# Two weight sums a stage later, a copy behind the norm, and a second buffer for the second sums

## The chip, the cores and the metric

The kernel runs on one core of a Trainium2 chip. The core has a matrix engine (TensorE, PE in the profile; its weight loads are the row PEld), a vector engine (VectorE, DVE), a scalar engine (ScalarE, ACT), a general engine (GpSimd, POOL) and DMA queues, which here are mostly filled by SyncE (SP). The metric is the time of one execution on the device in microseconds.

## What is computed

One layer of a hybrid backbone for 1024 latent tokens of width 1024, with 256 context tokens in front. Cut to what matters here:

```python
y_m = mlstm_merge(hm, om, mlstm_norm[l])                        # mLSTM heads, 512 columns
y_a = window_attention(q, k, v, k_ctx, v_ctx, attn_sink[l])     # 8 query heads, 512 columns
x = x + g_a * (concatenate([y_m, y_a]) @ w_out[l])              # the projection
h = modulate(rmsnorm(x, norm_ffn[l]), sh_f, sc_f)               # the norm
a, val = split(h @ w_up[l], 2)                                  # up projection, 2 x 2816 columns
x = x + g_f * ((gelu(dwconv(a)) * val) @ w_down[l])             # down projection
out = rmsnorm(x, final_norm)
```

## The kernel before, in words

Large matmuls are done in float32 by splitting each operand into a high part (a rounded copy, `fp32r`) and a low part (the difference), and adding three products. A split is therefore two steps: a copy, mostly on ScalarE, and a subtraction on VectorE (line 1193, the helper `sub`).

**Order.** From the attention on, the order of the work on TensorE, VectorE, ScalarE and GpSimd is that in which the program writes it (`manual_schedule`); each engine goes through its own list in order and waits where an input or a buffer is not ready. Lists of small steps, `more[t, i]`, are hung into the attention at stage t, place i, and run by `fill`.

**The attention** goes over 32 pairs (8 blocks of 128 tokens, 2 key heads, 2 pairs of query heads each), one pair per stage t, as a pipeline: at stage t, pair t has its scores made, pair t - 1 is normalised on GpSimd (`nrm`, line 1142), pair t - 2 is transposed on TensorE (`tr`, line 1154), copied (`hi`, line 1161), its low part made (`lo`, line 1167, tile `pl`) and multiplied with the values (`pv`, line 1177, tile `u`), and pair t - 3 finishes its products and is put together into `yT` (`y1`, lines 1182 and 1183; `y2`, lines 1188 and 1189). `u` has one buffer, so the next pair's `pv` waits for `y2`. Stages n = 32 and n + 1 only empty the pipeline. Beside it run the projection's products of the mLSTM half (`Wout`; its `add` is line 1092). At stage n, place 3, ahead of the pair's `pv`, VectorE makes three sums (lines 1252 and 1193) over the four quarters of block 0's up weights, which a DMA has put into `ym`; they go into `yS`, a part of the tile `yT`.

**The projection** of the attention half then goes over the tiles `order = [4, 1, 5, 2, 6, 3, 7]`; tile 0 was done in the attention. For each tile: 24 matmuls in two halves (`wout_n`, lines 307 to 309), an add to x (line 1383), the squares (`sq`, line 1393) and root (line 1398) on ScalarE, a reciprocal (line 1402) and the norm (`norm_b`, lines 1404, 1405 and 1407), transposes (`trans`, line 1419) and a move out of PSUM with scale and shift (`evac`, lines 1430 and 1432). The inputs `yT` of the tiles are split by `ysplit_h` and `ysplit_l`; the parts of the first three tiles have buffers of their own (`yh`, `yl`, three each), those of the others lie in free places of `hB`, the big pair of tiles for the up projection's token side.

**The up projection** multiplies 2 x 2 halves of tokens and of channels by seven products instead of eight, on sums and differences of the halves. The token sums of tile b and its partner b - 4 are `sum1` to `sum4`, split into the blocks T1 to T4 of `hB` (`split_t1` to `split_t4`, line 1443 for the copy); the plain blocks are B11, B21 and B22. `sum2` writes a tile `tb` of its own, which has one buffer and is read by `split_t2` and `sum4`. For tiles 6 and 7 (`late` and `last` in the code, with their partners 2 and 3), these steps stand after the loop, among the splits of block 0's weight sums (`wsplit_h`, line 1587). Behind them come five products of block 0, in this order: pf, pc (T1), pb (T2), pe (T3), pd (T4), and then block 1's.

Of the kernel before, what the change touches and what calls it, by code (L numbers as in the profile page):

```python
# [9 lines left out]
F32 = mybir.dt.float32  # L10
F32R = mybir.dt.float32r
# [7 lines left out]
P = 128  # L19
# [59 lines left out]
def build(tc, I, out, dbg=None):  # L79
    nc = tc.nc  # L80
    dbg = dbg or {}
    V, S, G, T = nc.vector, nc.scalar, nc.gpsimd, nc.tensor
# [41 lines left out]
    ym = rp.tile([P, NL, 512], F32, name="ym")  # L124
# [5 lines left out]
    hl = [hl_(0)]  # L130
# [13 lines left out]
    def load_split(src, w, rawf=None, split=True, alloc=True, now=range(2)):  # L144
        room = lambda: [st.tile([P, KT, XW], F32R, name=n, tag=n)[:].rearrange("p a b -> p (a b)")[:, :KT * w]
                        .rearrange("p (k f) -> p k f", k=KT) for n in ("wh", "wl")]
        hi, lo = room() if alloc else (None, None)
        raws = {}

        def load(q):  # L150
            raws[q] = rawf() if rawf else sr.tile([P, 4, XW], F32, name="wr", tag="wr")
            nc.sync.dma_start(raws[q][:, :, :w], src[:, 4 * q:4 * q + 4, :])

        def cut(q):
            ks, raw = slice(4 * q, 4 * q + 4), raws[q]
            S.copy(hi[:, ks, :w], raw[:, :, :w])
            V.tensor_tensor(out=lo[:, ks, :w], in0=raw[:, :, :w], in1=hi[:, ks, :w].bitcast(F32), op=ALU.subtract)

        if split:
            for q in range(2):  # L160
                load(q)
                cut(q)
            return hi, lo
        for q in now:
            load(q)

        def rest(qs=range(2)):
            nonlocal hi, lo
            if hi is None:
                hi, lo = room()  # L170
            for q in qs:
                cut(q)
            return hi, lo
        rest.load = load
        return rest
# [296 lines left out]
    order = (list(range(NCH)), [1, 0] + list(range(NCH - 1, NC - 1, -1)))  # L472
# [486 lines left out]
    n = 0  # L959
# [12 lines left out]
    for h in range(H):  # L972
# [3 lines left out]
        else:  # L976
            wq = [wkq]
            late = lambda: wq.append(load_split(I["w_q"][1], 256, lambda: pq.tile([P, 4, 256], F32, name="wr", tag="rga")))
# [66 lines left out]
    yslice = lambda b: next(v[:, t.index(b)] for t, v in yTa.items() if b in t)  # L1045
# [3 lines left out]
    t4 = pb_.enter_context(tc.tile_pool(name="t4", bufs=2, reuse_waits="tile"))  # L1049
# [7 lines left out]
    class Wout:  # L1057
# [32 lines left out]
        def add(self, n):  # L1090
            ns = slice(512 * n, 512 * n + 512)
            V.tensor_tensor(out=self.xb[:, ns], in0=self.po[:], in1=self.xb[:, ns], op=ALU.add)
            if n == 1:
                nc.sync.dma_start(x2_d[self.b][:], self.xb[:])
# [96 lines left out]
    order = [4, 1, 5, 2, 6, 3, 7]  # L1191
    ys = {}
    sub = lambda e, o, x, y: e.tensor_tensor(out=o, in0=x, in1=y, op=ALU.subtract)  # L1193

    def ysplit_h(b, eng=G, room=None):
        ys[b] = room or [t4.tile([P, 4, P], F32R, name=f"y{n}", tag=f"y{n}", bufs=3)[:] for n in "hl"]
        eng.copy(ys[b][0], yslice(b)) if eng is S else eng.tensor_copy(ys[b][0], yslice(b))

    def ysplit_l(b):
        sub(V, ys[b][1], yslice(b), ys[b][0].bitcast(F32))  # L1200
# [13 lines left out]
    more = collections.defaultdict(list)  # L1214
# [28 lines left out]
    n = len(pairs)  # L1243
# [4 lines left out]
    more[n - 5, 2] += [lambda: ysplit_l(order[0])]  # L1248
    more[n - 4, 0] += [lambda: ysplit_h(order[1], S)]
    more[n - 3, 0] += [lambda: ysplit_l(order[1])]  # L1250
    more[n - 2, 0] += [lambda: ysplit_h(order[2], S)]
    add = lambda e, o, x, y: e.tensor_tensor(out=o, in0=x, in1=y, op=ALU.add)
    yS = yTa[2, 0, 4, 1, 5][:].rearrange("p w k t -> p w (k t)")

    def load_0(to, h):
        nc.sync.dma_start(to, I["w_up"][0, :, 2 * h:2 * h + 2].rearrange("p q k f -> p q (k f)"))

    more[n - 11, 0] += [lambda: load_0(ym[:, 2:4], 0), lambda: load_0(ym[:, 4:6], 1)]
    more[n, 3] += [lambda: add(V, yS[:, 2], ym[:, 5], ym[:, 4]), lambda: sub(V, yS[:, 3], yS[:, 2], ym[:, 2]),
                   lambda: sub(V, yS[:, 1], ym[:, 3], yS[:, 3])]  # L1260

    attn = tc.manual_schedule(engines={mybir.EngineType.PE, mybir.EngineType.DVE, mybir.EngineType.Activation,
                                       mybir.EngineType.Pool})
# [4 lines left out]
    for t in range(n + 2):  # L1268
# [3 lines left out]
        if t in WOT:  # L1272
            k = 4 + WOT.index(t)
            room = [wop.tile([P, D], F32R, name=f"wo{n}{k}")[:] for n in "hl"]
# [70 lines left out]
    hB = [hbp.tile([P, 7, 4, 512], F32R, name=f"hB{i}") for i in range(2)]  # L1345
    tbk = ExitStack()
    tbp = tbk.enter_context(tc.tile_pool(name="tbp", bufs=1, side="right", reuse_waits="tile"))
    B11, B21, B22, T1, T2, T3, T4 = range(7)
# [19 lines left out]
    hns, rs, pts, raws, tbs = ({} for _ in range(5))  # L1368
    last = order[-1]
# [15 lines left out]
    def mean0(b):  # L1385
        V.tensor_scalar(out=rs[b][:, 2:3], in0=rs[b][:, 0:1], scalar1=1.0 / D, scalar2=EPS, op0=ALU.mult, op1=ALU.add)

    def sq(b, n, mean=True):
        if n == 0:
            hns[b] = t5.tile([P, D], F32, name="hn", tag="hn")  # L1390
            rs[b] = t5.tile([P, 3], F32, name="r2", tag="r2")
        ns = slice(512 * n, 512 * n + 512)
        S.activation(hns[b][:, ns], xs[b][:, ns], AF.Square, accum_out=rs[b][:, n:n + 1])
        if n == 1:
            if mean:
                run(1)
                mean0(b)
            S.activation(rs[b][:, 0:1], rs[b][:, 1:2], AF.Sqrt, bias=rs[b][:, 2:3], scale=1.0 / D)

    def norm_b(b, halves=False):  # L1400
        run(1)
        V.reciprocal(rs[b][:, 0:1], rs[b][:, 0:1])
        if halves:
            S.activation(hns[b][:, 0:512], xs[b][:, 0:512], AF.Copy, scale=rs[b][:, 0:1])
            V.tensor_scalar(out=hns[b][:, 512:D], in0=xs[b][:, 512:D], scalar1=rs[b][:, 0:1], scalar2=None, op0=ALU.mult)
        else:
            S.activation(hns[b][:], xs[b], AF.Copy, scale=rs[b][:, 0:1])
# [28 lines left out]
    def run(n=99):  # L1436
        for _ in range(min(n, len(held))):
            held.pop(0)()

    def split(b, blk, w, src, hi_eng=S):  # L1440
        ts = slice(b % 4 * P, b % 4 * P + P)
        hi, lo = (hB[i][:, blk:blk + w, :, ts] for i in range(2))
        (S.copy if hi_eng is S else hi_eng.tensor_copy)(hi, src)  # L1443
        return lambda: sub(V, lo, src, hi.bitcast(F32))


    def sum1(b):
        sub(V, raws[b - 4][:, 0], raws[b][:, 0], raws[b - 4][:, 0])

    def sum2(b):  # L1450
        tbs[b] = tbp.tile([P, 1, 4, P], F32, name="tb", tag="tb", bufs=1)
        sub(V, tbs[b][:, 0], raws[b][:, 1], raws[b - 4][:, 0])

    def sum3(b, e=V):
        sub(e, raws[b][:, 0], raws[b][:, 1], raws[b][:, 0])

    def sum4(b, e=V):
        sub(e, raws[b - 4][:, 1], raws[b - 4][:, 1], tbs[b][:, 0])

    split_b = lambda b: split(b, B22, 1, raws[b][:, 1:2])  # L1460
    split_t1 = lambda b: split(b, T1, 1, raws[b - 4][:, 0:1])
    split_t2 = lambda b: split(b, T2, 1, tbs[b][:])
    split_t3 = lambda b: split(b, T3, 1, raws[b][:, 0:1])
    split_t4 = lambda b: split(b, T4, 1, raws[b - 4][:, 1:2])
# [10 lines left out]
    add = lambda e, o, x, y: e.tensor_tensor(out=o, in0=x, in1=y, op=ALU.add)  # L1475
# [3 lines left out]
    fence.__enter__()  # L1479
    sq(0, 0)  # L1480
    sq(0, 1)
    for j in range(3, 7):
        ysplit_h(order[j], G, [hB[n][:, B22 + j - 3, :, 3 * P:4 * P] for n in range(2)])
    for j in range(2, 5):
# [3 lines left out]
    late = None  # L1488
    for i, b in enumerate(order):
# [20 lines left out]
        if pp is not None and pp < 4:  # L1510
# [4 lines left out]
            late = None  # L1515
            run(1)
        if pp is not None and pp >= 4:
# [6 lines left out]
            late = pp  # L1524
# [11 lines left out]
    evac(prev)  # L1536
    add1()
    late = pp
    lo_b = split_b(late)
    mean0(last)  # L1540
    lo3 = split(prev, B11, 2, raws[prev][:], V)
    sq(last, 1, False)
    sum1(late)
    norm_b(last, True)
    lo3()
    prod(ps_a, e0, 0, B11, True, True, None, c3)
    prod(ps_a2, e0, 1, B21, True, False, None, c3, range(2))
# [14 lines left out]
    f = ExitStack()  # L1562
# [20 lines left out]
    def wsplit_h(R, n):  # L1583
        src = (R[0] and R[0][:], R[1][:, 2:4], R[1][:, 0:2] if R[0] else r1[:], R[1][:, 4:5] if R[0] else yS[:, 1:2])[n]
        w = src.shape[1]
        wt = [fw.tile([P, w, 512], F32R, name=f"w{n}{w}", tag=f"w{n}{w}", bufs=5 if w == 2 else 2) for n in "hl"]
        S.copy(wt[0][:], src)  # L1587

        def lo():
            sub(V, wt[1][:], src, wt[0][:].bitcast(F32))  # L1590
            return wt
        return lo
# [5 lines left out]
    lo_b = split_b(last)  # L1598
# [9 lines left out]
    lo_2 = split_t2(late)  # L1608
    wS = wS()
    S.copy(ar0[:], ps_a[:])  # L1610
    lo_1()
    lo_2()
    sum3(late)
    sum4(late)
    sum2(last)
    lo_3, lo_4 = split_t3(late), split_t4(late)
    lo_2 = split_t2(last)
    wA = wsplit_h(R, 2)
    lo_2()
    sum3(last)  # L1620
    lo_5 = split_t3(last)
    lo_3()
# [8 lines left out]
                                                                    tag={"a": "a", "f": "b", "b": "b"}.get(n, "c"))  # L1631
# [118 lines left out]
    for i in range(1, NF):  # L1750
        last = i == NF - 1
# [175 lines left out]
    more = {}  # L1927
# [87 lines left out]
    for t, (p, ps, fresh) in enumerate(products):  # L2015
        for j in range(NP):
            n = NP * t + j
# [34 lines left out]
            if NP + 3 <= n < NP + 3 + NL:  # L2052
                b = n - NP - 3
# [17 lines left out]
    n = len(steps) - 3  # L2071
# [100 lines left out]
```

## Time and profile before

| | us |
|---|---|
| median of three runs | 1273.13 (1272.91 to 1273.3) |
| the profiled execution | 1274.79 |
| its span, first to last instruction | 1273.0 |
| TensorE busy | 1238.7 (97%) |
| VectorE busy | 974.5 (77%) |
| ScalarE busy | 638.0 (50%) |
| GpSimd busy | 188.0 (15%) |
| mean granted clock of TensorE | 0.997 |

Times in the profile count from the span's first instruction. A line of a timeline has the start, the duration, the engine, the line of the program, the operation, its output and inputs, shapes, and in brackets the engine's idle time before it with what ended that. The attention ends near 585 us, the projection near 630 us, and the up projection's own loop begins near 652 us. The projection's products before 585 us at lines 307 to 309 belong to the mLSTM half.

### The profile page before, as it was taken

The page shows a single profiled execution, that of the slowest core. Times are in us where ns is not written, and L with a number is a line of the kernel's source. Part 1 is how long each engine was busy: PE and PEld are TensorE (multiplying, and loading weights), DVE is VectorE, ACT ScalarE, POOL GpSimd, SP SyncE. Part 2 cuts the span into 40 slices and gives each one's busy share as a digit, 9 for nine tenths or more (in the row PEclk, how much of TensorE's full clock was granted, in tenths as well). Part 3 has the DMA queues.
Part 4 walks back from the last instruction along what each step waited for, and adds up shares of the span by engine and source line. Part 5 has one row for each costly group of instructions (what it writes and reads, how often), then busy time and mean ns, then how long its engine had stood idle before and what let it go on. Part 6 is the DMA issues. An engine that isn't in the chain of part 4 may idle for free.

```text
span 1273.0 us, 19254 instructions
## 1 busy us (share of the span) xinstructions
PE 1238.7 (97%) x7047; PEld 1062.6 (83%) x7047; DVE 974.5 (77%) x1691; ACT 638.0 (50%) x1309; POOL 188.0 (15%) x162
## 2 busy tenths in 40 slices
PE   6999999999999999999999999999999999999997
PEld 4799998989898888887877888888888888788886
DVE  4873687868787888788987877777777776867887
ACT  6732556464765877775844333333333333434435
POOL 1200000000000443221002331232231232001000
PEclk9999999999999999999999999999999999999999
DMA  9541544453255333104413322333322337975553
GB/s 356 186 125 35 142 129 145 117 170 92 79 166 171 133 117 117 51 33 136 146 50 116 115 100 92 108 108 108 108 99 91 108 119 268 342 255 179 196 194 135
DMA packets 90560, 176.17 MB, mean 138 GB/s; under 512 B 12954, under 2 KB 29538, under 8 KB 90466
## 3 DMA queue, kind: packets, MB, share of 16 engines
q1 hardware_dynamic: 90178, 174.15, 40.6%
q8 instruction: 56, 0.92, 0.3%
q10 hardware_dynamic: 288, 0.79, 0.2%
q14 instruction: 38, 0.31, 0.1%
HBM read 136.58 MB, written 38.33 MB: 137 GB/s over the span
## 4 chain that ended last, share of the span: by engine, by line
PE 76%; DVE 9%; ACT 6%; DMA 5%; issue 2%; POOL 1%; SPq 0%; ACTq 0%; DVEq 0%; POOLq 0%
PE pd L2009 14%; PE pa L1471 8%; PE pc L1471 8%; PE pp L588 7%; PE pe L1471 4%; PE pd L1471 4%; PE pb L1471 4%; PE u L1177 3%; PE pt L1154 2%; PE pv L307 2%; PE pv L309 2%; PE pv L308 2%; PE po L307 1%; PE po L309 1%; PE po L308 1%
## 5 line engine op out<-in xcount | busy, mean ns | idle before, releaser
L1587 ACT CAST wh<-Rb 128x1024 fp32r<-128x1024 f32 (+1 forms) x63 | 56.8, 904 | 144.4 <-PE pd L1471 77.3
L2009 PE MATMUL pd<-dh,al 128*128 128x512 f32 x296 | 115.4, 390 | 0.9 <-DVE al L1352 0.9
L2009 PE MATMUL pd<-dl,ah 128*128 128x512 f32 x296 | 115.3, 389 | 0.0
L2009 PE MATMUL pd<-dh,ah 128*128 128x512 f32 x296 | 115.1, 389 | 0.0
L1471 PE MATMUL pc<-hB,wh 128*128 128x512 f32 x344 | 105.6, 389 | 0.0
L1471 PE MATMUL pa<-hB,wh 128*128 128x512 f32 x336 | 103.7, 390 | 0.3 <-ACT sn L1668 0.2
L1193 DVE TENSOR_TENSOR wl<-Rb,wh 128x1024 fp32r<-128x1024 f32 (+1 forms) x63 | 65.8, 1046 | 39.2 <-ACT wh L1587 38.7
L1704 POOL TENSOR_TENSOR tt<-vt,tt 128x512 f32<-128x512 f32 x22 | 29.6, 1343 | 368.5 <-ACT tt L1698 368.5
L588 PE MATMUL pp<-hl,wh 128*128 128x512 f32 x256 | 79.3, 405 | 0.0
L307 PE MATMUL pv<-wh,hl 128*128 128x256 f32 x256 | 76.1, 297 | 0.8 <-ACT ym L601 0.8
L1471 PEld LDWEIGHTS pc<-hB,wh 128*128 128x128 f32 x344 | 64.6, 188 | 13.4
L1471 PEld LDWEIGHTS pa<-hB,wh 128*128 128x128 f32 x336 | 62.9, 188 | 14.1 <-ACT sn L1668 1.1
L309 PE MATMUL pv<-wh,hl 128*128 128x256 f32 x256 | 72.3, 283 | 0.0
L308 PE MATMUL pv<-wl,hl 128*128 128x256 f32 x256 | 72.3, 282 | 0.0
L2009 PEld LDWEIGHTS pd<-dh,al 128*128 128x128 f32 x296 | 55.6, 188 | 13.2 <-DVE al L1352 1.6
L1471 PE MATMUL pc<-hB,wl 128*128 128x512 f32 x172 | 66.4, 389 | 0.0
L1471 PE MATMUL pa<-hB,wl 128*128 128x512 f32 x168 | 65.4, 389 | 0.0
L2009 PEld LDWEIGHTS pd<-dl,ah 128*128 128x128 f32 x296 | 55.6, 188 | 11.7 <-DVE dl L1352 0.3
L2009 PEld LDWEIGHTS pd<-dh,ah 128*128 128x128 f32 x296 | 55.6, 188 | 11.6
L1161 ACT CAST ph<-pt 128x512 fp32r<-128x512 f32 (+1 forms) x88 | 46.2, 525 | 28.2 <-PE pt L1154 28.0
L1471 PE MATMUL pb<-hB,wh 128*128 128x512 f32 x176 | 54.0, 390 | 0.6 <-ACT hB L1443 0.6
L1131 DVE TENSOR_REDUCE nm<-sps 128x1 f32<-128x641 f32 (+1 forms) x64 | 50.3, 786 | 4.9 <-PE sps L1127 3.5
(1080 smaller groups left out, 3702.9 us busy)
## 6 DMA issues: line engine op xcount, KB each, us to landing
w<-in_w_ada_dram SPq DMA_DIRECT2D x64, 256.0 KB, 2.7
br<-in_w_down_dram SPq DMA_DIRECT2D x25, 512.0 KB, 5.2
ar<-act_s SPq DMA_DIRECT2D x44, 256.0 KB, 3.1
Ra<-in_w_up_dram SPq DMA_DIRECT2D x21, 512.0 KB, 3.6
Rb<-in_w_up_dram SPq DMA_DIRECT2D x21, 512.0 KB, 3.6
act_a<-tt SPq DMA_DIRECT2D x33, 256.0 KB, 2.0
act_s<-tt SPq DMA_DIRECT2D x33, 256.0 KB, 2.0
wr<-in_w_h_dram SPq DMA_DIRECT2D x16, 512.0 KB, 4.4
```

Source lines behind the costliest of these rows:

```text
L307: T.matmul(ps, st_hi, mv_hi, start=first, stop=False)
L308: T.matmul(ps, st_hi, mv_lo, start=False, stop=False)
L309: T.matmul(ps, st_lo, mv_hi, start=False, stop=last)
L588: T.matmul(pp[:, 512 * n:512 * n + 512], wkq[sw][:, kt, cs], hl[n][part][:, kt, :], start=kt == 0 and sw + part == 0, stop=kt == KT - 1 an ...
L1131: V.tensor_reduce(out=self.nm[:, j:j + 1], in_=self.sv[j], axis=AX.X, op=ALU.max, negate=True)
L1161: S.copy(self.ph[i][:, :w], self.pt[i][:, :w])
L1177: T.matmul(self.u[:], vv[:, c, self.g], part[i][:, kk * 2 * P:(kk + 1) * 2 * P], start=kb + m == 0, stop=kb == last and m == 1)
L1193: sub = lambda e, o, x, y: e.tensor_tensor(out=o, in0=x, in1=y, op=ALU.subtract)
L1471: T.matmul(ps[:, cols], wt[sw][:, j, kt * P:kt * P + P], hB[part][:, blk, kt, cols], start=first and n == 0, stop=last and n == len(seq) - ...
L1587: S.copy(wt[0][:], src)
L1704: G.tensor_tensor(out=self.tt[:, h2_], in0=self.vt[:], in1=self.tt[:, h2_], op=ALU.mult)
L2009: T.matmul(ps[:], ac[sa][:, js], w[sw], start=first and n == 0, stop=last and n == 2, skip_group_check=not fresh)
```

## The change

- At stage n of the attention one of the three weight sums stays; the other two run at stage n + 1, place 3.
- The low part of the third tile (`order[2]`, tile 5) goes to the place of T4's last tile in `hB[1]`; its high part keeps its buffer. So `yl` has two buffers instead of three, and `tb` has two instead of one.
- Behind the projection's last tile, the copy `split_b(late)` comes after the square, root and norm of the last tile instead of ahead of them.
- Among the last sums, `sum2(last)` and the copy `split_t2(last)` move up, ahead of `sum3(late)`; `sum4(late)` and `split_t4(late)` move down, behind the low part of T2.

```diff
     def ysplit_h(b, eng=G, room=None):
-        ys[b] = room or [t4.tile([P, 4, P], F32R, name=f"y{n}", tag=f"y{n}", bufs=3)[:] for n in "hl"]
+        room = room or [None, None]
+        ys[b] = [a if a is not None else t4.tile([P, 4, P], F32R, name=f"y{n}", tag=f"y{n}", bufs=3 if n == "h" else 2)[:]
+                 for a, n in zip(room, "hl")]
...
-    more[n - 2, 0] += [lambda: ysplit_h(order[2], S)]
+    yh2 = []
+    more[n - 2, 0] += [lambda: yh2.append(t4.tile([P, 4, P], F32R, name="yh", tag="yh", bufs=3)[:]),
+                       lambda: S.copy(yh2[0], yslice(order[2]))]
...
-    more[n, 3] += [lambda: add(V, yS[:, 2], ym[:, 5], ym[:, 4]), lambda: sub(V, yS[:, 3], yS[:, 2], ym[:, 2]),
-                   lambda: sub(V, yS[:, 1], ym[:, 3], yS[:, 3])]
+    more[n, 3] += [lambda: add(V, yS[:, 2], ym[:, 5], ym[:, 4])]
+    more[n + 1, 3] += [lambda: sub(V, yS[:, 3], yS[:, 2], ym[:, 2]), lambda: sub(V, yS[:, 1], ym[:, 3], yS[:, 3])]
...
     def sum2(b):
-        tbs[b] = tbp.tile([P, 1, 4, P], F32, name="tb", tag="tb", bufs=1)
+        tbs[b] = tbp.tile([P, 1, 4, P], F32, name="tb", tag="tb", bufs=2)
...
     sq(0, 1)
+    ys[order[2]] = [yh2[0], hB[1][:, T4, :, 3 * P:4 * P]]
...
     late = pp
-    lo_b = split_b(late)
     mean0(last)
     lo3 = split(prev, B11, 2, raws[prev][:], V)
     sq(last, 1, False)
     sum1(late)
     norm_b(last, True)
+    lo_b = split_b(late)
     lo3()
...
     lo_1()
+    sum2(last)
     lo_2()
+    lo_2 = split_t2(last)
     sum3(late)
-    sum4(late)
-    sum2(last)
-    lo_3, lo_4 = split_t3(late), split_t4(late)
-    lo_2 = split_t2(last)
+    lo_3 = split_t3(late)
     wA = wsplit_h(R, 2)
     lo_2()
+    sum4(late)
+    lo_4 = split_t4(late)
     sum3(last)
     lo_5 = split_t3(last)
     lo_3()
```

## The prediction

> **What bounds the kernel now.** I read the chain that ended last first, then TensorE's waits from 570 to 660 us, then the stretches around the longest wait, and last the engines' timelines there. In the chain:
>
> ```profile
> span 1273.0 us, 19254 instructions
> ...
> PE 76%; DVE 9%; ACT 6%; DMA 5%; issue 2%; POOL 1%; SPq 0%; ACTq 0%; DVEq 0%; POOLq 0%
> ```
>
> Three quarters of the chain is TensorE's own matmuls, so an edit on VectorE, ScalarE or a queue is worth only the TensorE idle time that it removes or adds. All three edits lie between 570 and 660 us. TensorE's waits there (total us, times, longest), longest first:
>
> ```profile
> PE u L1177 <- DVE yT L1189: 1.6, 1, 1.6
> PE pb L1471 <- ACT hB L1443: 0.6, 1, 0.6
> PE pt L1419 <- DVE hn L1405: 0.5, 1, 0.5
> PE pb L1471 <- DVE wl L1193: 0.3, 1, 0.3
> ```
>
> These four are the whole field. The first is the end of the attention, the third the last tile's norm, the second and fourth the weight and token sums ahead of the up projection. Now the stretches (columns: length, busy time of PE, PEld, DVE, ACT, POOL, granted clock, DMA share, GB/s):
>
> ```profile
> 575.53:578.94 3.41, 1.53 (x10) 1.01 (x9) 3.07 (x6) 0.33 (x1) 0.15 (x1) 1.00 0.44 98
> 578.94:582.36 3.42, 3.42 (x14) 3.02 (x14) 1.18 (x3) 1.15 (x4) 0.00 (x0) 0.50 0.53 208
> 582.36:585.77 3.41, 3.41 (x20) 2.93 (x20) 1.38 (x2) 0.82 (x3) 0.24 (x1) 1.00 0.00 0
> 642.10:645.50 3.40, 2.77 (x13) 1.96 (x12) 2.68 (x5) 2.79 (x4) 0.00 (x0) 1.00 0.45 129
> ```
>
> In the stretch with the 1.6 us wait TensorE is busy for 1.53 of 3.41 us, and in the next 3.42 us it is granted half its clock, busy throughout. So the wait costs twice: itself, and half of 3.42 us, 1.71 us, afterwards. The fourth row, with the 0.6 us wait, has 2.77 of 3.40 us busy and keeps the full clock.
>
> **Part 1: two of the three weight sums a stage later.** VectorE at stage n = 32, in order: two of block 0's sums, then the attention's work:
>
> ```profile
> 574.05 1.07 DVE L1193 TENSOR_TENSOR yT<-yT,ym 128x512 f32<-128x512 f32 x1
> 575.15 1.07 DVE L1193 TENSOR_TENSOR yT<-ym,yT 128x512 f32<-128x512 f32 x1
> 576.14 0.68 DVE L1167 TENSOR_TENSOR pl__7379<-pt,ph 128x512 fp32r<-128x512 f32 x1
> 576.74 0.27 DVE L1188 TENSOR_TENSOR yT<-u,ut 64x128 f32<-64x128 f32 x1
> 577.03 0.29 DVE L1189 TENSOR_TENSOR yT<-u,ut 64x128 f32<-64x128 f32 x1
> 577.35 0.69 DVE L1092 TENSOR_TENSOR x<-po,x 128x512 f32<-128x512 f32 x1
> 577.96 0.68 DVE L1167 TENSOR_TENSOR pl__7397<-pt,ph 128x512 fp32r<-128x512 f32 x1
> ```
>
> What these steps wait for, from ScalarE, and what TensorE does meanwhile:
>
> ```profile
> 574.09 0.59 ACT L1161 CAST ph<-pt 128x512 fp32r<-128x512 f32 x1 [0.86 <-PE pt L1154]
> 574.70 0.26 ACT L1182 COPY ut<-u 64x128 f32<-64x128 f32 x1
> 574.98 0.26 ACT L1183 COPY ut<-u 64x128 f32<-64x128 f32 x1
> ```
>
> ```profile
> 575.50 0.40 PE L309 MATMUL po<-woh,yml 128*128 128x512 f32 x1
> 577.47 0.47 PE L1177 MATMUL u<-ph,vv 128*128 128x256 f32 x2 [1.58 <-DVE yT L1189]
> ```
>
> Without the two sums, the low part pl can start when ph is there, 574.09 + 0.59 = 574.68, plus 0.03: 574.71. VectorE's steps start 0.60 us apart (576.14 to 576.74), so the halves of yT start at 575.31 and 575.60 (ut is done at 574.98 + 0.26 = 575.24) and end near 575.9 instead of 577.32. TensorE, done at 575.50 + 0.40 = 575.90, goes on near 576.05. The add at L1092 needs that same matmul, so it starts at 575.93 instead of 577.35: 1.42 us earlier, and the second pl, which TensorE wants next, with it. **Stall: 1.42 us.** Its upper bound is the whole wait, 1.58; its lower bound about 0.7, if the GpSimd work beside it slowed the two full-size steps, pl and the add, by 0.38 each as it does the sums:
>
> ```profile
> 573.59 0.99 POOL L1142 TENSOR_SCALAR p__7324<-p__7324,ss 128x512 f32<-128x512 f32 x1 [3.14 <-DVE ss L1139]
> 574.56 1.12 POOL L1142 TENSOR_SCALAR p__7349<-p__7349,ss 128x512 f32<-128x512 f32 x1
> ```
>
> (1.07 against 0.69 for the same kind of sum later, below.) I take 1.42, since those four steps read PSUM and took 0.68 and 0.29, with no sign of it.
>
> With the stall gone, the stretch from 575.53 has about 0.15 + 0.45 us of idle time left (the second pl comes 0.45 us after TensorE could take it), as near to the fourth stretch above as that row's 0.63. **Half clock: 1.71 us** goes too; bounds 0 and 1.71.
>
> Where the two sums land, at stage n + 1, VectorE has finished pl at about 577.2 and the next ph comes near 578.75: with TensorE at full clock, 0.23 us for the products of the second pl from 577.30 and 0.64 us for the transposes put the copy at 578.2, plus 0.59. GpSimd is done at 575.68, so the sums take about 0.7 us each and end near 578.6. They fit. If they took 1.07 us each, pl would come 0.6 us late, near 580.0; but it is wanted only after 12 more matmuls and 4 transposes, near 581.1. With that cover they cost nothing; without it, up to the 2.14 us that they take now.
>
> A transfer hangs on them: er's load was issued at
>
> ```profile
> 576.30 0.33 SPq L1256 DMA_DIRECT2D er<-in_w_up_dram  x1
> 576.68 0.42 SPq L1256 DMA_DIRECT2D r<-in_w_up_dram  x1
> 585.22 0.33 SPq L1094 DMA_DIRECT2D x_d<-x  x1
> ```
>
> right behind the second sum (575.15 + 1.07 = 576.22), whose ym it seems to overwrite. It and r1's load behind it on SP's queue will go at 578.7. er is wanted after the projection's first half tile, some 8 us later even with the gain; the two loads' stretch of DMA traffic lasts about 4 us. Cost 0, and the next entry of that queue, a store, comes at 585.22 - 3.13 = 582.1, still 3 us behind.
>
> The low part of the third projected tile moves from its own buffer into the place of T4's last tile in hB; it is the same VectorE step at the same place. T4 is written there only 40 us later. Cost 0, unless hB's second half is not free then (rival 4).
>
> **Part 2: a copy behind the norm.** ScalarE does the copy for B22, then the square; VectorE's reciprocal waits for both engines:
>
> ```profile
> 631.13 0.65 ACT L1443 CAST hB<-raw 128x512 fp32r<-128x512 f32 x1
> 631.64 0.67 ACT L1393 ACTIVATE hn<-x 128x512 f32<-128x512 f32 x1
> ```
>
> ```profile
> 631.90 0.68 DVE L1193 TENSOR_TENSOR raw<-raw 128x512 f32<-128x512 f32 x1
> 632.75 0.16 DVE L1402 RECIPROCAL r<-r 128x1 f32<-128x1 f32 x1 [0.17 <-ACT r L1398]
> ```
>
> Without the copy the square starts at about 631.2, when x is added, 0.4 us earlier; but VectorE's sum before the reciprocal holds it until 631.90 + 0.60 = 632.50. So the next late thing is VectorE, and the gain is 632.75 - 632.50 = **0.25 us** of the 0.5 us wait. The bounds are -0.1 and 0.42. The copy now runs after ScalarE's half of the norm, 0.5 us in an idle time before the evacuation of the last tile, which it may delay by 0.1 us (the lower bound). Its low part is a VectorE step that starts at 635.13, far behind.
>
> **Part 3: two buffers for the second sums.** VectorE's sum for T2 of the last tile had to follow the sum that reads the only buffer; now it comes before three other steps:
>
> ```profile
> 643.04 0.69 DVE L1193 TENSOR_TENSOR tb<-er,raw 128x512 f32<-128x512 f32 x1
> 644.42 0.69 DVE L1193 TENSOR_TENSOR hB<-tb,hB 128x512 fp32r<-128x512 f32 x1 [0.68 <-ACT hB L1443]
> ...
> 649.95 0.69 DVE L1193 TENSOR_TENSOR hB<-raw,hB 128x512 fp32r<-128x512 f32 x1 [0.69 <-ACT hB L1443]
> 650.90 1.23 DVE L1193 TENSOR_TENSOR wl<-Ra,wh 128x1024 fp32r<-128x1024 f32 x1 [0.26 <-ACT wh L1587]
> ```
>
> TensorE's 0.6 us wait for this tile goes: the copy for T2 moves from 643.77 to about 641.6, two steps of 0.60 us before TensorE wants it. On VectorE the 0.68 us and some 0.12 us before 643.04 go; the 0.69 us for T4 and the 0.26 us behind it stay, since sum, copy and low part still follow one another there. So VectorE comes out 0.80 us earlier, with part 2's shift 1.05. That is the number that counts, because the next wait is on VectorE:
>
> ```profile
> 656.46 0.50 PE L1471 MATMUL pb<-hB,wl 128*128 128x512 f32 x1 [0.30 <-DVE wl L1193]
> ```
>
> TensorE could gain at most 0.47 + 0.62 + 0.30 = 1.39 us over parts 2 and 3; T4's copy, near 648.9, comes just when the product d wants it. **Parts 2 and 3 together: 1.05 us**, between 0.25 and 1.39. Behind 656 us TensorE runs almost without waits to the end, so all of it should arrive.
>
> **Sum.** 1.42 + 1.71 + 1.05 = 4.18 us. The profiled execution took 1274.79 us (span 1273.0 and 1.79 around it) and would become 1270.6. It is 1.66 us above the median of the timed runs, 1273.13; from that median the same sum gives 1268.95.
>
> **Rivals.** (1) The timed runs have no half-clock stretch to lose. For it: the profiled execution is 1.66 us longer than they are, nearly the 1.71 us. Against it: a profile may lengthen an execution by itself, and the three timed runs lie within 0.4 us, which a stretch that comes and goes would not leave. Then 1.42 + 1.05 = 2.47 us are gained: 1270.66, on the edge of what can be told. The Trainium skill (TensorE: Matmul & The Clock Gate, "HAM oscillation — how this bites in real kernels") says that idle gaps above about 3.4 us are what brings the half clock. By that rule a 1.58 us wait would not cause it and its removal would save only the wait: the same 1270.66. The trace speaks against the rule here, with half clock right after 1.58 us of waiting and 45% busy time. The same page ("What's actually happening") calls the window free-running, about 3.4 us long, as the 3.42 us row shows; with the edges elsewhere the wait could be split over two windows.
>
> (2) The last third does not arrive: ScalarE's copies in the new order come too late for T3 or T4, and only the 0.25 us of the norm stay. For it: T4's copy has no slack. Then 1.42 + 1.71 + 0.25 = 3.38: 1269.75.
>
> (3) The sums are not what holds the attention's end, and TensorE's wait passes to ph or to the add at L1092. Against it: all inputs of pl were there 1.4 us before it began. Then only parts of 0.25 us remain: 1272.9, no change.
>
> (4) Slower: the first write to hB's second half, now 0.85 us earlier on VectorE, has to wait for attention tiles under it. Behind it in VectorE's queue stands the reciprocal for tile 0, then its norm and the transposes on TensorE, which have no slack, so each us of waiting counts in full. GpSimd's first write to the other half,
>
> ```profile
> 585.53 2.75 POOL L1197 CAST hB<-yT 128x512 fp32r<-128x512 f32 x4 [9.85 <-issue]
> ```
>
> went before that store of 585.22 can have landed, which speaks against a wait for it. It decides from 4.2 us on: a tile that holds hB for 7 us would give 1273.13 - 4.18 + 7 = 1275.95.
>
> **How the numbers follow.** Forecast 0.50, rival 1 0.27, rival 2 0.10, rival 3 0.07, rival 4 0.06. I predict 1269.0. The range goes down to 1273.13 - 1.58 - 1.71 - 1.39 = 1268.45 and up to rival 1 with part 3 missing, 1273.13 - 1.42 - 0.25 = 1271.46; it leaves out rivals 3 and 4. About 0.2%, 2.55 us, is what can be told from no change. Faster by more: the forecast, half of rival 1 and 0.07 of rival 2, 0.71. Within: the other half of rival 1, the rest of rival 2 and rival 3, 0.23. Slower 0.06.
>
> **What would show it.** Right: in the profile after, the wait of u for yT below 0.3 us; no stretch at 0.50 of the clock between 570 and 600; both sums after the pl of stage n; the wait for T2's copy gone, the wait of pt for hn about 0.2, and a wait of pb for wl still there. Wrong: half clock that stays with a short wait; a new wait of TensorE for hB (T4) or of VectorE at its first hB write; a span less than 3 us shorter.

## The result, and the profile after

Nineteen runs of each gave a median of 1270.49 us (1268.48 to 1272.22) after the change and 1272.6 us (1271.16 to 1275.62) before it, a ratio of 0.9983 (95% interval 0.9977 to 0.9990). That is 2.1 us less, inside the predicted range of 1268.45 to 1271.46, but 1.5 us above the forecast of 1269.0 and just inside the 0.2% that I had called no change. The forecast's rival 1 had 1270.66. One later run of the kernel before took 1319.76 us and is left out of the ratios and means below.

The profiled execution after the change took 1271.14 us, against 1274.79: 3.65 us less, where the forecast's sum for one profiled execution was 4.18. From its page, the span and the shares of the chain that ended last:

```profile
span 1269.3 us, 19257 instructions
...
PE 78%; DVE 9%; ACT 6%; DMA 4%; issue 2%; POOL 1%; SPq 0%; ACTq 0%; DVEq 0%; POOLq 0%
```

TensorE's waits from 560 to 660 us after the change (total us, times, longest):

```profile
PE u L1177 <- ACT p__7266 L1135: 0.6, 1, 0.6
PE pt L1423 <- DVE hn L1409: 0.3, 1, 0.3
PE pb L1475 <- DVE wl L1193: 0.3, 1, 0.3
PE u L1177 <- DVE pl__7394 L1167: 0.3, 1, 0.3
PE u L1177 <- DVE pl__7346 L1167: 0.2, 1, 0.2
PE u L1177 <- DVE pl__7289 L1167: 0.2, 1, 0.2
PE u L1177 <- DVE yT L1189: 0.2, 1, 0.2
```

The wait of u for yT went from 1.6 to 0.2 us, the 0.6 us of pb for T2's copy is gone, pt for hn went from 0.5 to 0.3, and pb for wl is still there at 0.3. (The first row lies ahead of the change.) VectorE at stages n and n + 1, and GpSimd's last step there:

```profile
574.94 0.69 DVE L1167 TENSOR_TENSOR pl__7376<-pt,ph 128x512 fp32r<-128x512 f32 x1 [0.69 <-ACT ph L1161]
575.54 0.27 DVE L1188 TENSOR_TENSOR yT<-u,ut 64x128 f32<-64x128 f32 x1
575.83 0.29 DVE L1189 TENSOR_TENSOR yT<-u,ut 64x128 f32<-64x128 f32 x1
576.16 0.69 DVE L1092 TENSOR_TENSOR x<-po,x 128x512 f32<-128x512 f32 x1
576.76 0.68 DVE L1167 TENSOR_TENSOR pl__7394<-pt,ph 128x512 fp32r<-128x512 f32 x1
577.36 0.68 DVE L1193 TENSOR_TENSOR yT<-yT,ym 128x512 f32<-128x512 f32 x1
578.08 0.69 DVE L1193 TENSOR_TENSOR yT<-ym,yT 128x512 f32<-128x512 f32 x1
579.10 0.69 DVE L1167 TENSOR_TENSOR pl__7417<-pt,ph 128x512 fp32r<-128x512 f32 x1 [0.33 <-ACT ph L1161]
```

```profile
574.79 0.69 POOL L1142 TENSOR_SCALAR p__7348<-p__7348,ss 128x512 f32<-128x512 f32 x1
```

Now pl waits for ph, not for the sums; the sums take 0.68 and 0.69 us instead of 1.07, with GpSimd done, and the next pl still waits 0.33 us for ScalarE behind them. TensorE there, and the clock that it was granted (columns as in the prediction):

```profile
575.71 0.40 PE L309 MATMUL po<-woh,yml 128*128 128x512 f32 x1
576.27 0.47 PE L1177 MATMUL u<-ph,vv 128*128 128x256 f32 x2 [0.17 <-DVE yT L1189]
```

```profile
575.20:578.61 3.41, 2.96 (x19) 2.27 (x18) 3.33 (x7) 0.98 (x3) 0.29 (x1) 1.00 0.00 0
578.61:582.03 3.42, 3.42 (x21) 2.90 (x20) 2.37 (x6) 1.56 (x4) 0.00 (x0) 1.00 0.57 147
```

The half clock of before is gone from this place. (The mean granted clock of this execution is 0.997 all the same: it has a half-clock stretch from 15.41 to 18.83 us, which the trace of before has not, and the end, without matmuls, is at half clock in both.) er's load is issued later, behind the second sum, as expected, and no engine waits for it from 585 to 640 us:

```profile
578.85 0.33 SPq L1260 DMA_DIRECT2D er<-in_w_up_dram  x1
579.23 0.42 SPq L1260 DMA_DIRECT2D r<-in_w_up_dram  x1
```

Part 2 on ScalarE and VectorE:

```profile
628.48 0.66 ACT L1397 ACTIVATE hn<-x 128x512 f32<-128x512 f32 x1
...
630.06 0.72 ACT L1408 ACTIVATE hn<-x,r 128x512 f32<-128x512 f32 x1 [0.50 <-DVE r L1406]
630.69 0.60 ACT L1447 CAST hB<-raw 128x512 fp32r<-128x512 f32 x1
```

```profile
629.26 0.69 DVE L1193 TENSOR_TENSOR raw<-raw 128x512 f32<-128x512 f32 x1
629.87 0.15 DVE L1406 RECIPROCAL r<-r 128x1 f32<-128x1 f32 x1
```

The square comes first now, and the reciprocal follows VectorE's sum with no idle time, while ScalarE now waits 0.50 us for it: VectorE is the later of the two, as predicted. Part 3 on VectorE:

```profile
638.22 0.69 DVE L1193 TENSOR_TENSOR tb<-er,raw 128x512 f32<-128x512 f32 x1
638.82 0.69 DVE L1193 TENSOR_TENSOR hB<-tb,hB 128x512 fp32r<-128x512 f32 x1
...
646.15 0.69 DVE L1193 TENSOR_TENSOR hB<-raw,hB 128x512 fp32r<-128x512 f32 x1 [0.69 <-ACT hB L1447]
647.10 1.23 DVE L1193 TENSOR_TENSOR wl<-Ra,wh 128x1024 fp32r<-128x1024 f32 x1 [0.26 <-ACT wh L1592]
```

The 0.68 us ahead of T2's low part is gone; the 0.69 us for T4 and the 0.26 us behind it stay.

### The profile page after: what moved, and what is told of

It reads as the page before. It is cut to its first block, busy times and chain, and to the rows that moved or that the text cites. A ratio compares the mean times of both kernels' runs of the same rounds, so it can differ in the third digit from the quotient of the medians.

```text
span 1269.3 us, 19257 instructions
## 1 busy us (share of the span) xinstructions
PE 1237.0 (97%) x7047; PEld 1061.1 (84%) x7047; DVE 973.6 (77%) x1691; ACT 637.7 (50%) x1309; POOL 187.6 (15%) x162
## 4 chain that ended last, share of the span: by engine, by line
PE 78%; DVE 9%; ACT 6%; DMA 4%; issue 2%; POOL 1%; SPq 0%; ACTq 0%; DVEq 0%; POOLq 0%
PE pd L2015 14%; PE pa L1475 8%; PE pc L1475 8%; PE pp L588 7%; PE pe L1475 4%; PE pd L1475 4%; PE pb L1475 4%; PE u L1177 3%; PE pt L1154 2%; PE pv L307 2%; PE pv L309 2%; PE pv L308 2%; PE po L307 1%; PE px L309 1%; PE po L309 1%
## 5 line engine op out<-in xcount | busy, mean ns | idle before, releaser
L832 DVE SCALAR_TENSOR_TENSOR acc<-w,sp,acc 128x512 f32<-128x512 f32 x62 | 46.1, 743 | 10.6 <-DMA w<-in_w_ada_dram 10.6
```

What stands on the lines that cost most here:

```text
L832: V.scalar_tensor_tensor(out=acc[:], in0=w2[:], scalar=cr, in1=acc[:], op0=ALU.mult, op1=ALU.add)
```

## How the traces are compared

A time of a whole run is a blunt tool here. The matmul that starts at 385.42 us in the profile of before, long ahead of anything that was changed, starts between 2.22 us earlier and 0.36 us later in the other thirteen traces of this study, whatever the kernel. So the start of the same matmul was compared between each trace and the profile of before. The table has what each stretch gained (negative) or lost between two such matmuls, in us. The columns, by the times of before: 571.8 to 577.5 (the wait at stage n), 577.5 to 584.4 (behind it, where before had half clock), 628.6 to 633.7 (the last tile's norm), 633.7 to 646.2 (the last sums), 646.2 to 799.6 (the up projection's first blocks).

```
trace                 wait   behind    norm    sums   blocks
changed kernel       -1.43    -1.61   -0.13   -0.94   +0.02
after_again          -1.43    -1.61   -0.30   -0.99   +0.08
e1_sums_only         -1.42    -1.59   +0.03   -0.02   -0.02
e2_tail_only         -0.02    -1.61   -0.27   -0.99   +0.04
e3_filled_wait       -0.02    -1.60   +0.17   -0.03   -0.02
e4_copy_only          0.00    -0.02   -0.30    0.00   -0.06
e5_buffers_only      -0.01    -1.60   +0.17   -0.99   +0.05
e6_sums_twice        +1.44    +0.68   +0.16   -0.02   -0.03
e9_two_waits_more    -1.42    -1.62   -0.38   -0.92   +0.72
e10_block1_sums      -1.43    -1.61   -0.21   -0.94   +0.10
before_look1         +0.01    -1.59   -0.02   -0.02   +0.02
before_look2         -0.01     0.00   -0.02   -0.01   +0.01
before_look3         -0.01    -1.59   -0.04    0.00   -0.04
```

From 584.4 to 628.6 us only two traces moved by more than 0.05 us, `e3` (+0.27) and `e6` (+1.04). Behind 799.6 us the traces part near 1075 us alone, by -0.31 to +0.59 us, unchanged kernels among them.

## The experiments

Theories, as they stood after the result: A, the wait is always worth 1.4 us and the half clock 1.7 us only in some executions; B, half clock in every execution of before; C, all of the gain comes from the last sums. D (on when half clock follows) and E (on `e9`) came later, and the expectations that test them say what they are.

**Part 1 alone** (`e1_sums_only`).

```diff
-    more[n, 3] += [lambda: add(V, yS[:, 2], ym[:, 5], ym[:, 4]), lambda: sub(V, yS[:, 3], yS[:, 2], ym[:, 2]),
-                   lambda: sub(V, yS[:, 1], ym[:, 3], yS[:, 3])]
+    more[n, 3] += [lambda: add(V, yS[:, 2], ym[:, 5], ym[:, 4])]
+    more[n + 1, 3] += [lambda: sub(V, yS[:, 3], yS[:, 2], ym[:, 2]), lambda: sub(V, yS[:, 1], ym[:, 3], yS[:, 3])]
```

> The kernel before with part 1 alone (the two weight sums at stage n + 1). Theory A (the wait is always worth 1.4 us, the half-clock stretch 1.7 us only in those executions in which it falls): in the trace no wait of u for yT over 0.3 us, no half clock between 570 and 600 us; the timed median 1.4 to 2.3 us below before. Theory B (the half-clock stretch is in every execution of before): 3.1 us below. Theory C (the whole measured gain comes from the last sums): less than 0.6 us below.

Measured: median 1270.94 us against 1272.77, ratio 0.9987 (0.9977 to 0.9998), 1.8 us less. The trace has -1.42 in the wait and nothing in the norm and the sums. C falls; A fits; B's 3.1 us lies outside the interval (0.25 to 2.9).

**Parts 2 and 3 alone** (`e2_tail_only`): the changed kernel with the diff above undone.

> The changed kernel with the two weight sums back at stage n: parts 2 and 3 alone. Theories A and B: TensorE's wait of 1.6 us for yT is back, the waits of pb for T2's copy is gone, that of pt for hn is 0.2 to 0.3 us; the timed median 0.9 to 1.1 us below before. Theory C: about 2 us below. The trace is also a second look at whether half clock follows the 1.6 us wait: B says it does, A says perhaps.

Measured: 1271.08 us against 1272.77, ratio 0.9988 (0.9979 to 0.9997). The trace gives -0.27 and -0.99. It also shows something new: the 1.6 us wait is there, and no half clock follows.

```profile
571.18:574.59 3.41, 2.41 (x16) 1.74 (x14) 3.34 (x5) 1.70 (x4) 2.08 (x2) 1.00 0.02 5
574.59:578.01 3.42, 2.55 (x17) 2.21 (x18) 1.72 (x5) 0.62 (x2) 0.00 (x0) 1.00 0.85 256
```

These two rows are stretches of the grid on which this trace's clock changes lie. All changes of the granted clock within a trace lie whole multiples of 3.413 us apart (in before at 15.75, 578.95, 582.36 and 1268.44 us, which is 165, 166 and 367 steps from the first), and the grid lies differently in each execution. Here an edge at 574.59 cuts the wait in two, and each part leaves TensorE busy for over two thirds. B falls.

**The wait filled with work** (`e3_filled_wait`).

```diff
+    def busy():
+        sp_ = pSs[1][0].tile([P, 1024], F32, name="sps", tag=pSs[1][1])
+        for _ in range(6):
+            T.matmul(sp_[:, 0:512], QTs[NL - 1][:, 0], kT2[0][:, 0, 0:512], start=True, stop=True)
+
+    more[n, 2] += [busy]
```

> The kernel before with six 128x512 matmuls, whose results nobody reads, in TensorE's 1.6 us wait at stage n (1.4 us of work); the sums stay at stage n. The wait itself stays, only TensorE is not idle in it. Theory A: no half clock, the products behind it start when they did (within 0.1 us), the timed median 0 to 0.9 us below before (half clock is in fewer than half of the executions of before). Theory B: 1.7 us below.

Measured: 1272.67 us against 1272.77, ratio 1.0000 (0.9992 to 1.0009). In the trace TensorE runs the six matmuls and then waits 0.20 us:

```profile
574.11 1.53 PE L1265 MATMUL sps<-kT,QT 128*128 128x512 f32 x6
575.84 0.47 PE L1177 MATMUL u<-ph,vv 128*128 128x256 f32 x2 [0.20 <-DVE yT L1189]
```

The wait's stretch is as long as before (-0.02) and the clock stays full:

```profile
573.84:577.25 3.41, 2.91 (x15) 2.08 (x14) 3.12 (x6) 0.40 (x1) 0.21 (x1) 1.00 0.37 96
577.25:580.66 3.41, 3.41 (x21) 2.91 (x21) 1.87 (x4) 1.70 (x4) 0.00 (x0) 1.00 0.54 211
```

That is as A says, and B's 1.7 us lies outside. That the filling is what kept the clock full can be read from the place of the grid. The gap that the six matmuls fill would have begun 0.44 us behind an edge. In three traces of the unfilled wait with half clock (`before`, and further below `e4_copy_only` and `before_look2`) it begins 0.36, 0.47 and 0.27 us behind one, so half clock was to be expected here without the filling. It is one trace. This trace also lost 0.45 us from 591 to 634 us, nearly all of it behind 628 us, for no cause that was found.

**The copy alone** (`e4_copy_only`).

```diff
     late = pp
-    lo_b = split_b(late)
...
     norm_b(last, True)
+    lo_b = split_b(late)
```

> The kernel before with part 2 alone (the copy for B22 behind the last tile's norm). All theories: the wait of pt for hn goes from 0.5 to about 0.2 us, the copy follows ScalarE's half of the norm; 0.25 us less, which the timed median can hardly tell from nothing. If the copy delays the evacuation instead, the products from B22 on start no earlier. Also a third look at whether half clock follows the 1.6 us wait.

Measured: 1272.38 us against 1272.77, ratio 0.9998 (0.9989 to 1.0008), no difference that the runs can tell. The trace has -0.30 in the norm and no loss behind it. Half clock followed the wait here, in whose stretch TensorE was busy for 1.52 us.

**Part 3 alone** (`e5_buffers_only`): `e2_tail_only` with that copy back in its old place.

> The kernel before with part 3 alone (two buffers and the new order of the last sums, the third tile's low part in hB). Theory A: TensorE's 0.6 us wait of pb for T2's copy is gone, the 0.5 us wait of pt for hn and the 0.3 us wait of pb for wl stay, products from block 1 on are 0.8 us earlier against the start of the projection's last tile; timed median 0.8 us below before. Theory C (the last sums carry all of the measured gain): 2 us below. Where the 1.6 us wait falls inside one stretch of the 3.41 us grid, half clock follows; where an edge of the grid cuts it, not.

Measured: 1272.24 us against 1272.81, ratio 0.9997 (0.9989 to 1.0006). The trace has -0.99 in the sums, somewhat more than the 0.8 expected, and the 1.6 us wait without half clock:

```profile
573.13:576.54 3.41, 1.83 (x11) 1.25 (x10) 3.33 (x6) 1.65 (x4) 1.54 (x2) 1.00 0.09 13
```

The last sentence of the expectation is wrong as it stands: the wait, from 574.87 to 576.46 us, lies inside this one stretch, and half clock does not follow.

**The sums twice** (`e6_sums_twice`).

```diff
+    more[n, 3] += more[n, 3][-2:]
```

> The kernel before with the two weight sums at stage n made twice over (the same values): TensorE's wait grows from 1.6 us to about 3.7 us. Theory D (half clock follows when TensorE is busy for less than some half of one stretch of a 3.41 us grid that lies differently in each execution): now half clock follows wherever the grid lies, so the timed median is 2.1 us + 0.5 to 1 us above before, 2.6 to 3.2 us, or more where two stretches are slow. If half clock had nothing to do with the wait: 2.1 us above, and mean clocks as before.

Measured: 1275.86 us against 1272.81, ratio 1.0023 (1.0012 to 1.0034), 3.05 us more. The wait grew to 3.0 us, not 3.7: GpSimd had ended, and the second round of sums took 0.69 us each. On the grid:

```profile
574.12:577.53 3.41, 1.12 (x7) 0.64 (x5) 3.31 (x6) 1.03 (x3) 0.90 (x1) 1.00 0.00 0
577.53:580.95 3.42, 2.70 (x13) 2.73 (x13) 1.85 (x5) 0.00 (x0) 0.00 (x0) 0.50 0.77 231
580.95:584.36 3.41, 3.41 (x11) 2.73 (x11) 1.59 (x4) 1.69 (x4) 0.00 (x0) 0.50 0.19 76
```

One third busy, and two stretches at half clock. The mean granted clock of its seven runs was 0.99686, against 0.99768 in 78 runs of before. The two slow stretches are as D says. The 3.05 us say less than they seem to: the wait grew by 1.4 us and not by 2.1, and 1.04 us of this trace's loss lies in the projection, where VectorE waits 1.39 us for a late load of x.

**The changed kernel again** (`after_again`).

> The changed kernel once more, beside the others on one chip. Theory A with half clock in about half of the executions of before: 1.4 + 0.8 + 1.05 = 3.2 us below before. If part 1 or part 3 gives some of it back later: about 2 us below. No half clock between 570 and 600 us in the trace, wherever the grid lies.

Measured: 1270.62 us against 1272.81, ratio 0.9984 (0.9975 to 0.9992), 2.2 us less, with the same steps in the trace as the first time.

**The kernel before, three more traces** (`before_look1` to `before_look3`), unchanged.

> The kernel before, unchanged: one more place of the 3.41 us grid. Theory D: half clock follows the 1.6 us wait if the grid's stretch that holds most of it has TensorE busy for less than some share between 0.45 (half clock so far) and 0.54 (none so far) of it, else not; in about a quarter of executions.

> The kernel before, unchanged, as in the look before it: half clock after the 1.6 us wait only where the grid's stretch around it is busy for less than 0.45 to 0.54.

> The kernel before, unchanged, as in the two looks before it: half clock after the 1.6 us wait only where the grid's stretch around it is busy for less than 0.45 to 0.54.

The stretch of the grid that holds most of the wait, and the one behind it, in `before_look2`, `before_look1` and `before_look3`:

```profile
574.34:577.75 3.41, 1.56 (x11) 1.12 (x10) 2.97 (x6) 0.25 (x1) 0.05 (x1) 1.00 0.47 113
577.75:581.17 3.42, 3.42 (x15) 2.93 (x14) 1.18 (x3) 1.33 (x4) 0.00 (x0) 0.50 0.49 194
```

```profile
573.77:577.18 3.41, 1.83 (x12) 1.28 (x11) 3.33 (x6) 1.35 (x4) 1.25 (x2) 1.00 0.13 28
577.18:580.59 3.41, 3.10 (x21) 2.63 (x21) 1.74 (x5) 1.51 (x4) 0.00 (x0) 1.00 0.82 280
```

```profile
573.97:577.38 3.41, 2.22 (x14) 1.57 (x12) 3.33 (x6) 1.69 (x4) 2.02 (x2) 1.00 0.02 5
577.38:580.80 3.42, 2.74 (x18) 2.38 (x19) 1.73 (x4) 0.78 (x2) 0.00 (x0) 1.00 0.89 280
```

Seven traces now have the same wait of 1.56 to 1.60 us. Half clock followed in the three in which TensorE was busy for 1.52, 1.53 and 1.56 us of one stretch, and not in the four in which the emptiest stretch had 1.83, 1.83, 2.22 and 2.41 us. The wait begins 0.27 to 0.47 us behind an edge in the three, and 1.47 to 2.41 us behind one in the four. Apart from `e6`, the fourteen traces have no other stretch below 1.83 us and no other half clock from 20 to 1255 us. So at this place the line lies between 46% and 54%.

As a rule for the whole program a busy share alone does not hold. Behind the last matmuls of `e9` and of `e10`, both below, the clock stays full after 1.54 and 1.51 us of work:

```profile
1258.89:1262.31 3.42, 1.54 (x7) 0.94 (x5) 2.23 (x5) 1.65 (x5) 0.00 (x0) 1.00 0.56 208
1262.31:1265.72 3.41, 0.00 (x0) 0.00 (x0) 1.35 (x3) 1.85 (x5) 0.00 (x0) 1.00 0.59 217
```

The profile's busy time counts modelled ends of matmuls, and there the work stands in one piece at the start of the stretch. Whether the share, the place of the gap in its stretch or another measure of work decides is not shown.

**Two more waits** (`e9_two_waits_more`, and one of its two edits alone, `e10_block1_sums_first`).

```diff
     sq(last, 1, False)
-    sum1(late)
     norm_b(last, True)
+    sum1(late)
...
-    add(V, B.u2[:], ps0["b"][:], ar0[:])
     sums_v(R)
-    add(V, ar0[:], ps_a2[:], ar0[:])
+    add(V, B.u2[:], ps0["b"][:], ar0[:])
     add(V, u2b[:], ps0["f"][:], B.u2[:])
     W[1] = wsplit(R, 1)
+    add(V, ar0[:], ps_a2[:], ar0[:])
```

`e10_block1_sums_first` has the second half of it only.

> The changed kernel with two of its remaining waits worked on: the sum for T1 behind the last tile's norm instead of ahead of the reciprocal, and block 1's weight sums ahead of block 0's adds, with one of those adds behind block 1's split. The 0.3 us wait of pb for wl goes, that of pt for hn falls by 0.1 us; 0.4 us earlier than the changed kernel from block 1 on, and 3 to 3.6 us below before. If the adds that come later now hold a buffer of TensorE's, a new wait of pb or pa of up to 0.6 us takes its place.

> The changed kernel with only one of e9's two edits: block 1's weight sums ahead of block 0's adds, one of those adds behind block 1's split; the sum for T1 stays ahead of the reciprocal. Theory E (e9 lost because VectorE, which has hardly any idle time from 628 to 656 us, came out 0.3 us later): without e9's other edit T4's copy is as early as in the changed kernel, the 0.3 us wait of pb for wl goes, no wait of pd or pc takes its place, and TensorE is 0.3 us earlier to the end than in the changed kernel. If the block 1 order itself was at fault, pc waits for av again and the end is as late as e9's.

Measured: `e9` 1269.71 us against 1272.81, ratio 0.9978 (0.9968 to 0.9988); `e10` 1269.61 against 1272.91, ratio 0.9977 (0.9968 to 0.9985). Both medians are lower than the changed kernel's, by less than their intervals can tell from it, and the traces show no gain. `e9` won 0.38 us in the norm and lost 0.72 in the blocks. In `e10` TensorE is 0.46 us earlier by 663 us and loses 0.56 again before 800 us, so it ends no earlier than the changed kernel. Its waits from 560 to 700 us:

```profile
PE pa L1475 <- ACT sn L1674: 0.4, 2, 0.2
...
PE pc L1475 <- DVE av L1479: 0.3, 1, 0.3
```

The wait of pb for wl is gone, and pc waits for av in its place. Theory E is half right. From 634 to 656 us `e9` gained 0.61 us less than the changed kernel, with a 0.3 us wait of pd for T4's copy, and `e10`, without that edit, had all of it: this part of `e9`'s loss is T4's copy. But E also had `e10` gain to the end, and there it fails: in both traces the block 1 order brings about 0.5 us near 657 us and loses it again near 669 us. VectorE's av of block 1 starts 1.69 us earlier in `e10` than in the changed kernel's trace, but by 656 us all of TensorE's work is 1.81 us earlier there: that chain did not get shorter, so TensorE only runs into it. Neither is shown to be a better version.

## Why the prediction came out as it did

**Stall, 1.42 us:** 1.42 to 1.43 in every trace without the sums at stage n, by the mechanism given: pl waits for ph, L1092 follows 1.4 us earlier, and pl of the next product with it. GpSimd did not slow pl, which ran beside it in 0.69 us. The reason given for that was no evidence, though: in the profile of before GpSimd had ended at 575.68 us, ahead of all four steps that showed "no sign of it". The trace after has them side by side (pl 574.94 to 575.63 us, GpSimd 574.79 to 575.48). The sums fitted in at stage n + 1 with 0.33 us to spare.

**Parts 2 and 3, 1.05 us:** 0.13 and 0.30 for the norm (0.25 predicted), 0.94 and 0.99 for the sums (0.80), together 1.07 and 1.29 in the two traces of the changed kernel. I had undersized the sums by about 0.15 us, and VectorE was what counted, as said: the 0.3 us wait of pb for wl remained. (The four waits called the whole field were not quite all: u waited 0.3 and 0.2 us for pl as well, and still does.)

**Half clock, 1.71 us:** 1.6 us where it was there; this is the step that failed, not in its size but in its chance. I took it into the forecast in full, because three timed runs lay within 0.4 us of one another. That the runs spread over 4.5 us was seen only with nineteen of them. Three traces of the seven with the wait have half clock, and the mean granted clock of the runs says much the same: 0.99768 in 78 runs of before and 0.99817 in the 30 of the changed kernel, a difference of 0.00049, where one half-clock stretch makes 1.71 of 1273 us, 0.00134. So about 36% of before's executions had it. This is a rough estimate: the clocks come in three decimals and also move with half clock at the program's start and end, and the difference has a 95% interval that puts the share between 12% and 61%. The profile that the prediction was made from happened to be one of those. Rival 1 was the right one, though not as worded: the timed runs have some, not none. That the median came as near the forecast as 1.5 us is part luck: the gain was 2.1 us where 4.18 were forecast, and the three runs that it was taken off had a median 0.53 us above that of the nineteen.

The Trainium skill (TensorE: Matmul & The Clock Gate, "HAM oscillation — how this bites in real kernels") gives idle gaps of over about 3.4 us as what brings half clock. Here 1.56 us was enough in some executions. Its other statement ("What's actually happening"), a free-running window of about 3.4 us, is what all fourteen traces agree with: 3.41 us, with a different place in each.

**What stays open.** The steps of the traces add up to 1.43 + 1.07 to 1.29, about 2.6 us, and 36% of 1.6 us on top makes some 3.2 us, or 2.8 to 3.6 us by the interval of that share. The means of the runs, 1272.93 (97 of before) and 1270.48 (30 of the changed kernel), differ by 2.45 us, give or take 0.45. The two ranges just meet, with 0.7 us between their middles; whether that is chance, or something given back in executions that no trace here shows, was not settled. Rivals 2, 3 and 4 did not occur: the gain of the last sums arrived without a wait for T3 or T4, the wait at stage n did not pass to another step, and VectorE's first write to hB's second half waited for nothing.

## What to carry to other kernels

A step that nobody needs soon is worth moving if it stands ahead of one that the busiest engine waits for; read from the profile what the freed step waits for next, since that sets the gain. A short wait on TensorE can cost more than itself by the clock, but only in the executions in which the clock's grid catches it: count that cost by its chance, read several traces before giving it a whole place in the sum, and compare the starts of the same matmul between traces where the runs' totals scatter. An edit that only brings TensorE earlier, where VectorE's chain stays as long, is given back at the next product.

## What was not expected of the hardware

Half clock depended on where a 3.41 us grid lay in that execution. Around the wait, 1.52 to 1.56 us of work in one stretch was followed by half clock in the next 3.41 us, 1.83 us was not, and 1.12 us was followed by two such stretches; with the gap filled the clock stayed full. At the program's end 1.51 and 1.54 us of work was not followed by it. VectorE's subtractions with both inputs in SBUF took 1.07 us beside GpSimd's multiplications and 0.69 us without; pl, with an input from PSUM, took 0.68 to 0.69 us in both cases.
